# A two-layer hybrid decoder trunk: one written order for three engines through both routers

## The chip, the cores and the metric

The kernel runs on one core of one Trainium2 chip. The metric is the device time of one execution in microseconds (us). The kernel before took 904.0 us, the median of three runs (903.87 to 907.41). Its profiled execution took 905.78 us by the same clock and shows a span of 904.1 us, at a mean granted TensorE clock of 0.985.

## The reference, cut to what matters

256 tokens of width 1024 pass through two layers. Each layer is a mixer (layer 0 an mLSTM block, layer 1 a block-sparse attention) and a mixture of experts with 16 experts, two per token, chosen inside one group of four. Every sublayer ends in a layer normalisation.

```
x = layer_norm(ALPHA * x + gate * mixer(modulate(x)), ln_g, ln_b)
# router, on h = modulate(x, shift, scale)
probs  = softmax(h @ w_router)
scores = (probs + b_router).reshape(T, 4, 4)
group  = argmax over groups of the sum of the two best scores in the group
idx    = the two best experts of that group;  w = probs[idx] / sum(probs[idx])
# experts
y = sum over idx of w * ((silu(h @ w_gate[e]) * (h @ w_up[e])) @ w_down[e])
x = layer_norm(ALPHA * x + gate * y, ln_g, ln_b)
```

The shift, scale and gate vectors come from one condition vector through a matrix `w_ada` of 14 column blocks of 1024.

## The kernel before, in words

**The stream of weights.** All weights come from HBM in pieces of 0.5 MB, issued by SP in the order of their use into a ring of buffers (20 pieces, and 18 more during a mixture of experts). A piece is issued when the buffer it takes has been read for the last time. The experts' weights of one layer are 192 pieces.

**The end of a mixer.** The last part of the output projection (`y` in layer 0, `by` in layer 1) adds into four PSUM banks, one for each half of each of the two 128-token tiles. In layer 0 it is 48 matmuls of 128x512, from `wout_part` with h == 3 (L939 on); in layer 1 it stands just ahead of the last call of `moe` (L1539 on). Every product is three matmuls of high and low parts (`mm3`, L274 to L276). Written ahead of them is `before_moe` (L473): it finishes three condition vectors and folds the router's weights with one of them. On DVE, `adacc` sums a condition vector in eight passes over 128x1024 (L362), then PE sums over the partitions (`adaps`, L368), ACT copies the result (`mr`) and PE turns it (`adat`, L348). `wrt` (DVE, L483) is the router's weights times scale and shift; `rb` (PE, L485) sums it over the partitions, and `wr` (L488) is the folded router. `adag` (L452, L455) are the banks of a gate row. `ada_all` drives what is left of these sums.

**The router** (`moe`, L974 on). The gated sum into the residual `xt` (L547, L548), the statistics of the normalisation, the transposes `th` with their copies `xT`, the logits `pr`, `lr`, `pl`, `lg`, the exponentials `pexp` on ACT (they need the Exp table of ACT, loaded at `preload`, L536), and some thirty small DVE steps that end in `mask` (L1065). From the mask PE counts the places (`pp`, L1071), DVE forms the places (`pos`) and the one-hot matrices (`onehot`, L1089), and PE gathers the tokens of four experts (`ga`) from the normalised rows, which are split into a high part `xh` (ACT) and a low part `xl` (DVE, L1017). The gathered tokens are scaled into `xe` (L525 on ACT, L523 on DVE, two blocks of 128 columns each in turn), and the first gate products `pg` follow, 32 matmuls. They are the first that read the experts' weights. `lnps` are banks with the normalisation's rows; from them DVE forms the start of the residual sum in eight passes (L1335, L1336). `mxi` is the number of tokens of the fullest expert; every engine reads it for a branch (L1338) to a part for overflowing experts.

**What sets the order.** A scheduler orders the instructions of each engine by readiness and priority. Where `pinned` is set on an engine's wrapper (`Ordered`, L117), an instruction keeps its place in program order against the others, and its line shows as L135. In the kernel before only PE is pinned, from the first gather (`ga`) on through the experts. The end of the mixer and the router are the scheduler's.

Of the kernel before, what the change touches and what calls it, by code (L numbers as in the profile page):

```python
# [21 lines left out]
NT = S // P  # L22
# [6 lines left out]
E = 16  # L29
# [128 lines left out]
def _body(ctx, tc, x, w_ada, a_w_in, a_wq, a_wk, a_wv, a_w_out, b_w_kv, b_wq, b_wo, moe_w_gate, moe_w_up,  # L158
          moe_w_down, pc, rows, cst, out):
    nc = tc.nc  # L160
    V, A, T = [Ordered(tc, e) for e in (nc.vector, nc.scalar, nc.tensor)]
# [3 lines left out]
    small = ctx.enter_context(tc.tile_pool(name="small", bufs=2))  # L165
# [10 lines left out]
    def bankB(name):  # L176
        return psB.tile([P, 512], F32, tag="B", name=name)
# [11 lines left out]
    def C(name):  # L189
        g, o, w = CS[name]  # L190
        return cs[g][:, o:o + w]
# [15 lines left out]
    count = [0]  # L207
# [336 lines left out]
    def add_gated(t, o, n, y, gate, name, dst=xt):  # L544
        c = slice(o, o + n)
        tmp = small.tile([P, 512], F32, tag="lntmp", name=f"lntmp{name}{t}{o}")[:, 0:n]
        V.tensor_tensor(tmp, y, gate[:, c], op=OP.mult)  # L547
        V.tensor_tensor(dst[:, t, c], dst[:, t, c], tmp, op=OP.add)  # L548

    def ln_stats(src, t, name):  # L550

        st = small.tile([P, 4, 6], F32, tag="lnst", name=f"lnst{name}{t}")
        mv = small.tile([P, 2], F32, tag="lnmv", name=f"lnmv{name}{t}")
        rs = small.tile([P, 1], F32, tag="lnrs", name=f"lnrs{name}{t}")
        for i in range(4):
# [5 lines left out]
    def normalise(src, t, st, on_act=False):  # L561
        if on_act:
            nb = small.tile([P, 1], F32, tag="lnnb", name=f"lnnb{count[0]}_{t}")
            V.scalar_tensor_tensor(nb, st[0], -1.0, st[1], op0=OP.mult, op1=OP.mult)
            return A.activation(xt[:, t, :], src[:, t, :], AF.Identity, bias=nb, scale=st[1])
# [373 lines left out]
    def wout_part(h, w, ahl):  # L939
        ws = {}  # L940
        late = pe.tile([P, 2, 2, 512], F32R, tag="hh", name="wlate") if h == 3 else None
        for hf in range(2):
            for k in range(0, 4, 2):
                pump()
                pump()
                ws[k, hf], ws[k + 1, hf] = split(wsp, w[hf][:, k:k + 2, :], f"wo{h}_{k}{hf}", late if (k, hf) == (0, 0) else None)
            if h < 3:
                for t in range(NT):
                    for k in range(4):
                        mm3(yA[t][hf], tuple(a[:, k, P * t:P * t + P] for a in ahl), ws[k, hf], h == 0 and k == 0, False)  # L950
        if h == 3:
            gate = before_moe(0)
            ada_all()
            for t in range(NT):
                for hf in range(2):
                    for k in range(4):
                        mm3(yA[t][hf], tuple(a[:, k, P * t:P * t + P] for a in ahl), ws[k, hf], False, k == 3)
            return gate
# [15 lines left out]
    def moe(layer, y, gate1, last):  # L974
        ln0 = 2 * layer
        jm = 6 * layer + 3
        with ExitStack() as mc:
# [8 lines left out]
            xh = pm.tile([P, NT, D], F32R, name=f"xh{layer}")  # L986
            xl = pm.tile([P, NT, D], F32R, name=f"xl{layer}")
            lg = pm.tile([P, NT, E], F32, name=f"lg{layer}")
            for t in range(NT):
                for h in range(2):  # L990
                    add_gated(t, 512 * h, 512, y[t][h], gate1, f"m{layer}")
                for h in range(2):
                    pt = bankB(f"th{layer}_{t}{h}")
                    for k in range(4):
                        T.transpose(pt[:, P * k:P * k + P], xt[:, t, 512 * h + P * k:512 * h + P * k + P], ident)
                    A.copy(xT[:, t, 4 * h:4 * h + 4, :], pt.rearrange("p (k s) -> p k s", k=4))
                pr = bankB(f"pr{layer}_{t}")
# [3 lines left out]
                lr = small.tile([P, P], F32, tag="cv", name=f"lr{layer}_{t}")  # L1001
                V.tensor_copy(lr, pr[:, 0:P])
                T.matmul(pl[:, E * t:E * t + E], lr, C("selr"), start=True, stop=True)
                st = ln_stats(xt, t, f"m{layer}")
                V.scalar_tensor_tensor(lg[:, t, :], pl[:, E * t:E * t + E], st[1], rb[:, E:], op0=OP.mult, op1=OP.add)
                if t:
                    end = preload(AF.Exp)
                normalise(xt, t, st, t == 0)

            def split_x(t):  # L1010
                with tc.issue_after(end):
                    A.copy(xh[:, t, :], xt[:, t, :])

            def low_part(t):
                for h in range(2):
                    c = slice(512 * h, 512 * h + 512)
                    V.tensor_tensor(xl[:, t, c], xt[:, t, c], xh[:, t, c].bitcast(F32), op=OP.subtract)  # L1017

            split_x(0)

            def sm(nm, shape, dt=F32):
                return pm.tile([P] + shape, dt, name=f"{nm}_{layer}")

            def bc(t, n):
                return t.unsqueeze(len(t.shape)).to_broadcast(list(t.shape) + [n])
# [4 lines left out]
            ss = sm("ss", [NT, E])  # L1030
            V.tensor_reduce(s1, lg, axis=AX.X, op=OP.max, negate=True)
            for t in range(NT):
                end = A.activation(pe[:, t, :], lg[:, t, :], AF.Exp, bias=s1[:, t:t + 1], accum_out=s2[:, t:t + 1]).ins
            split_x(1)

            rows_ = [ln_bank(ln0, q, h, bankA) for h in range(2) for q in range(2)]
            gate = gate_rows(jm + 2)
# [16 lines left out]
            V.tensor_reduce(gs.rearrange("p t g -> p (t g)"), pairs, axis=AX.X, op=OP.max)  # L1054
            gl = sm("gl", [NT, NG, 3])
            gn = sm("gn", [NT, NG])
            losses(gl, gs)
            V.tensor_reduce(gn, gl, axis=AX.X, op=OP.add)
            el = sm("el", [NT * NG, 4, 3])
            en = sm("en", [NT * NG, 4])  # L1060
            losses(el, g4)
            V.tensor_reduce(en, el, axis=AX.X, op=OP.add)
            V.tensor_scalar(en, en, 1.5, None, op0=OP.is_lt)
            mask = sm("mask", [NT, E], BF16)
            V.scalar_tensor_tensor(mask.rearrange("p t (g j) -> p (t g) j", g=NG), bc(gn.rearrange("p t g -> p (t g)"), 4), 0.5, en,  # L1065
# [36 lines left out]
            wide = sm("wide", [NT, P + 2 * E], F32R)  # L1102
            for t in range(NT):
                V.tensor_copy(wide[:, t, 0:P], ident)
# [430 lines left out]
            wps[k, hf], wps[k + 1, hf] = split(wsp, w[hf](k), f"bo{hf}_{k}", None if hf else late[(k - 4) // 2])  # L1535
    gate = before_moe(1)
    ada_all()
    for t in range(NT):
# [46 lines left out]
```

## Time and profile before

| | |
|---|---|
| median of three runs | 904.0 us (903.87 to 907.41) |
| profiled execution: its time, its span | 905.78 us, 904.1 us |
| PE busy | 858.2 us (95%) |
| DVE, ACT busy | 529.1 us (59%), 331.4 us (37%) |
| weights and inputs read | 316.53 MB, 351 GB/s over the span |
| the chain that ended last | PE 40%, DMA 10%, DVE 3%, ACT 2% |

Busy shares are means over stages with different limits. PE counts as busy while it holds a matmul, also when its clock is low or when it goes no faster than the weights come. So the stages are read one by one: layer 0's mixer ends near 293 us, its experts run from 317 to 522 us, mixer 1 to 662 us, its experts from 681 us to the end.

### The profile page before, as it was taken

How to read it: one execution, taken by the hardware profiler on the slowest of the kernel's cores; microseconds unless marked ns; L12 is line 12 of the kernel's file. 1: busy time of each engine (PE TensorE's matmuls, PEld its weight loads, DVE VectorE, ACT ScalarE, POOL GpSimd, SP SyncE). 2: the span in 40 equal slices, each digit the busy share in tenths (PEclk: the TensorE clock that was granted, in tenths of full speed). 3: DMA queues.
4: the chain of work that ended last, by engine and by line, in shares of the span. 5: the costliest groups of instructions: out<-in, count | busy, mean ns of one | idle time of the engine just before them, and what ended most of it. 6: DMA issues, size and time to landing. Idle time of an engine off the chain costs nothing.

```text
span 904.1 us, 13441 instructions
## 1 busy us (share of the span) xinstructions
PE 858.2 (95%) x5049; PEld 533.3 (59%) x5052; DVE 529.1 (59%) x963; ACT 331.4 (37%) x550; POOL 7.8 (1%) x21
## 2 busy tenths in 40 slices
PE   8998999998999799999999889999979999999994
PEld 4887998786887434334343369877754443434332
DVE  2469997587878824332333289999983323333317
ACT  3458665357564411112111036576652111101020
POOL 0020000000000000000000000000000000000000
PEclk9999999999999899999999999999989999999998
DMA  9999886798868999999999999976997999999993
GB/s 326 393 386 355 293 330 205 273 411 324 307 227 275 381 333 407 407 407 406 408 406 407 377 387 412 400 284 238 361 338 262 407 407 407 407 407 407 407 400 121
DMA packets 161921, 318.56 MB, mean 352 GB/s; under 512 B 10120, under 2 KB 28168, under 8 KB 161848
## 3 DMA queue, kind: packets, MB, share of 16 engines
q1 hardware_dynamic: 161704, 317.42, 93.5%
q8 instruction: 42, 0.69, 0.3%
q14 instruction: 31, 0.25, 0.1%
q10 hardware_dynamic: 144, 0.20, 0.1%
HBM read 316.53 MB, written 1.05 MB: 351 GB/s over the span
## 4 chain that ended last, share of the span: by engine, by line
PE 40%; DMA 10%; DVE 3%; ACT 2%; issue 1%; DVEq 0%; SPq 0%; ACTq 0%
PE py L135 8%; PE pg L135 8%; PE pu L135 7%; DMA w<-in_moe_w_up_dram 3%; DMA w<-in_moe_w_down_dram 3%; PE ga L135 3%; PE po L135 2%; DMA ada<-in_w_ada_dram 2%; DMA w<-in_moe_w_gate_dram 1%; PE bo L1477 1%; PE bk L275 1%; PE by L274 1%; PE bk L276 1%; PE bk L274 1%; PE by L276 1%
## 5 line engine op out<-in xcount | busy, mean ns | idle before, releaser
L1238 DVE SCALAR_TENSOR_TENSOR yl<-py,wsl,yh 128x512 fp32r<-128x512 f32 x28 | 21.0, 750 | 171.2 <-ACT yh L1237 171.2
L135 PE MATMUL py<-w,aT 128*64 128x512 f32 (+1 forms) x576 | 118.3, 548 | 1.8 <-DMA w<-in_moe_w_down_dram 1.8
L135 PE MATMUL pu<-w,xe 128*64 128x512 f32 x512 | 118.8, 596 | 0.2 <-DMA w<-in_moe_w_up_dram 0.2
L135 PE MATMUL pg<-w,xe 128*64 128x512 f32 x512 | 116.1, 596 | 0.0
L362 DVE SCALAR_TENSOR_TENSOR adacc<-ada,pk,adacc 128x1024 f32<-128x1024 f32 x70 | 89.4, 1278 | 0.4
L135 PEld LDWEIGHTS py<-w,aT 128*64 128x64 f32 x576 | 41.3, 137 | 74.4 <-issue 58.8
L135 PEld LDWEIGHTS pu<-w,xe 128*64 128x64 f32 x512 | 36.1, 137 | 67.5 <-issue 61.2
L135 PEld LDWEIGHTS pg<-w,xe 128*64 128x64 f32 x512 | 34.8, 137 | 63.9 <-issue 58.9
L1204 ACT COPY aT<-aT 128x512 f32<-128x512 f32 x16 | 9.4, 586 | 139.5 <-PE aT L135 139.5
L547 DVE TENSOR_TENSOR lntmpe<-po,gate 128x512 f32<-128x512 f32 x56 | 36.1, 685 | 41.3 <-PE po L135 41.3
L1237 ACT ACTIVATE yh<-py,wsl 128x512 fp32r<-128x512 f32 x28 | 19.2, 687 | 84.2 <-PE py L135 84.2
L525 ACT ACTIVATE xe<-ga,coef 128x256 f32<-128x256 f32 x32 | 16.1, 562 | 73.0 <-PE ga L135 63.0
L274 PE MATMUL z<-hh,wz 128*128 128x256 f32 x128 | 36.7, 287 | 0.0
L276 PE MATMUL z<-hh,wz 128*128 128x256 f32 x128 | 36.2, 283 | 0.0
L275 PE MATMUL z<-hl,wz 128*128 128x256 f32 x128 | 36.1, 282 | 0.0
L548 DVE TENSOR_TENSOR xt<-xt,lntmpe 128x512 f32<-128x512 f32 x56 | 36.0, 683 | 0.0
L1197 DVE TENSOR_TENSOR a<-a,pu 128x512 f32<-128x512 f32 x16 | 11.0, 689 | 36.4 <-PE pu L135 20.3
L135 PE MATMUL ga<-onehot,xh 128*128 128x256 f32 x128 | 31.8, 327 | 0.0
L135 PE MATMUL xm<-hh,win 128*128 128x256 f32 x144 | 28.9, 290 | 0.7 <-ACT hh L135 0.7
L1192 ACT ACTIVATE a<-pg 128x512 f32<-128x512 f32 x16 | 9.6, 597 | 52.2 <-PE pg L135 52.2
L135 PEld LDWEIGHTS ga<-onehot,xh 128*128 128x128 f32 x128 | 25.3, 223 | 5.6 <-DVE xt L548 4.1
L135 PE MATMUL ga<-onehot,xl 128*128 128x256 f32 x128 | 27.7, 283 | 0.0
(387 smaller groups left out, 1892.9 us busy)
## 6 DMA issues: line engine op xcount, KB each, us to landing
w<-in_moe_w_gate_dram SPq DMA_DIRECT2D x128, 512.0 KB, 10.2
w<-in_moe_w_up_dram SPq DMA_DIRECT2D x128, 512.0 KB, 10.2
w<-in_moe_w_down_dram SPq DMA_DIRECT2D x128, 512.0 KB, 10.2
ada<-in_w_ada_dram SPq DMA_DIRECT2D x112, 512.0 KB, 9.2
win<-in_a_w_in_dram SPq DMA_DIRECT2D x16, 512.0 KB, 8.4
wz<-in_a_w_in_dram SPq DMA_DIRECT2D x16, 512.0 KB, 7.5
wout<-in_a_w_out_dram SPq DMA_DIRECT2D x16, 512.0 KB, 10.1
wv<-in_a_wv_dram SPq DMA_DIRECT2D x8, 512.0 KB, 5.8
```

The costliest lines, as they stand in the source:

```text
L135: return self.tc.keep_in_program_order(f(*a, **kw))
L274: T.matmul(ps, l[0], r[0], start=start, stop=False, skip_group_check=True)
L275: T.matmul(ps, l[0], r[1], start=False, stop=False, skip_group_check=True)
L276: T.matmul(ps, l[1], r[0], start=False, stop=stop, skip_group_check=True)
L362: V.scalar_tensor_tensor(acc, w, c, acc, op0=OP.mult, op1=OP.add)
L525: A.activation(dst, ps, AF.Identity, bias=sh[:, k:k + 1], scale=sc[:, k:k + 1])
L547: V.tensor_tensor(tmp, y, gate[:, c], op=OP.mult)
L548: V.tensor_tensor(dst[:, t, c], dst[:, t, c], tmp, op=OP.add)
L1192: A.activation(a, pg, AF.Silu)
L1197: V.tensor_tensor(a, a, pu, op=OP.mult)
L1237: A.activation(yh, py, AF.Copy, scale=wsl[:, b:b + 1])
L1238: V.scalar_tensor_tensor(yl, py, wsl[:, b:b + 1], yh.bitcast(F32), op0=OP.mult, op1=OP.subtract)
```

## The change

From the last products of a mixer to the high and low parts of the router's weights `W`, the instructions of PE, DVE and ACT keep the order in which the code writes them. For PE the flag is set ahead of the last products of each mixer; for DVE and ACT from the first gated sum of the router to `wide`. Inside, some steps are written in other places: the two tiles' transposes, logits and sums stand interleaved; the normalisation of `xt` is written after the exponentials (tile 1) and after the first one-hot (tile 0); tile 0's high part is formed by ACT straight from the unnormalised row, with bias and scale; the low parts and the normalisation of `W` stand behind the first one-hot; the copies of the identity into `wide` stand ahead of the router; the order of two groups of comparisons is exchanged.

```diff
@@ wout_part, h == 3 (and the same line ahead of the last products of mixer 1)
             gate = before_moe(0)
             ada_all()
+            T.pinned = True
             for t in range(NT):
@@ moe
+            for t in range(NT):
+                V.tensor_copy(wide[:, t, 0:P], ident)
+            V.pinned = A.pinned = T.pinned = True
...
             for t in range(NT):
                 for h in range(2):
                     add_gated(t, 512 * h, 512, y[t][h], gate1, f"m{layer}")
+                    if (t, h) == (1, 0):
+                        V.reciprocal(rs[0], rs[0])
+                        V.scalar_tensor_tensor(nb, mv[0][:, 0:1], -1.0, rs[0], op0=OP.mult, op1=OP.mult)
+                    for i in range(2 * h, 2 * h + 2):
+                        V.bn_stats(st[t][:, i, :], xt[:, t, 256 * i:256 * i + 256])
+                V.bn_aggr(mv[t], st[t])
+                if t == 0:
+                    A.activation(rs[0], mv[0][:, 1:2], AF.Sqrt, bias=epsc)
...
+            A.activation(rs[1], mv[1][:, 1:2], AF.Sqrt, bias=epsc)
+            A.activation(warm, epsc, AF.Exp)
...
-                if t:
-                    end = preload(AF.Exp)
-                normalise(xt, t, st, t == 0)
...
-            split_x(0)
...
             for t in range(NT):
-                end = A.activation(pe[:, t, :], lg[:, t, :], AF.Exp, ...)
-            split_x(1)
+                A.activation(pe[:, t, :], lg[:, t, :], AF.Exp, ...)
+            normalise(xt, 1, (mv[1][:, 0:1], rs[1]))
+            A.activation(xh[:, 0, :], xt[:, 0, :], AF.Identity, bias=nb, scale=rs[0])
+            A.copy(xh[:, 1, :], xt[:, 1, :])
...
-            V.tensor_reduce(s1, W, axis=AX.X, op=OP.add)
-            V.reciprocal(s1, s1)
-            V.tensor_tensor(W, W, bc(s1, E), op=OP.mult)
...
+            onehot(0)
+            normalise(xt, 0, (mv[0][:, 0:1], rs[0]))
             low_part(0)
-            placed = onehot(0)
-            with tc.issue_after(placed):
-                low_part(1)
+            placed = low_part(1)
+            V.tensor_reduce(s1, W, axis=AX.X, op=OP.add)
+            V.reciprocal(s1, s1)
+            V.tensor_tensor(W, W, bc(s1, E), op=OP.mult)
...
+            V.pinned = A.pinned = T.pinned = False
```

PE's queue at the end of mixer 0, in the kernel before (av, axc: the activations' parts; wlate, wo: parts of the output weights; adaps and adat are the next condition vector's sum and turn):

```order
L455 MATMUL adag_1_2998<-mr_1781,pick 128x512
L274 MATMUL y_0_2289<-wlate,av_2851 128x512
...
L275 MATMUL y_1_2290<-wo_21_2990,av_2851 128x512
L485 MATMUL rb_3009<-wrt_3006,ones 128x256
L276 MATMUL y_1_2290<-wo_21_2990,axc_2852 128x512
...
L276 MATMUL y_1_2292<-wo_21_2990,axc_2852 128x512
L368 MATMUL adaps_3022<-adacc_2926,ones 32x256 x4
L502 MATMUL lnps_0_0_3235<-lnr,pick 128x512
L348 MATMUL adat_3029<-cs,mr_3027 128x128 x2
```

The same place in the changed kernel:

```order
L455 MATMUL adag_1_2998<-mr_1781,pick 128x512
L485 MATMUL rb_3009<-wrt_3006,ones 128x256
L368 MATMUL adaps_3022<-adacc_2926,ones 32x256 x4
L348 MATMUL adat_3029<-cs,mr_3027 128x128 x2
L135 MATMUL y_0_2289<-wlate,av_2851 128x512 x2
L135 MATMUL y_0_2289<-wlate,axc_2852 128x512
...
L135 MATMUL y_1_2292<-wo_21_2990,axc_2852 128x512
L135 MATMUL th_00_3174<-cs,xt 128x128 x4
```

`rb`, `adaps` and `adat` stood among and behind the 48 `y` products; now they stand ahead of all of them.

PE's queue at the end of mixer 1, in the kernel before (kT_wo, vv_wo, bo: parts of the output weights):

```order
L276 MATMUL by_1_6169<-bo_2_6253,ol__5275 128x512
L274 MATMUL by_1_6171<-bo_2_6253,oh__5274 128x512
...
L485 MATMUL rb_6352<-wrt_6349,ones 128x256
L368 MATMUL adaps_6356<-adacc_6210,ones 32x256 x4
...
L276 MATMUL by_1_6171<-bo_6_6331,ol__5275 128x512
```

In the changed kernel:

```order
L455 MATMUL adag_1_6340<-mr_5465,pick 128x256 x2
L485 MATMUL rb_6352<-wrt_6349,ones 128x256
L368 MATMUL adaps_6356<-adacc_6210,ones 32x256 x4
L135 MATMUL by_0_6168<-kT_wo,oh__5274 128x512 x2
L135 MATMUL by_0_6168<-kT_wo,ol__5275 128x512
...
L135 MATMUL by_1_6171<-bo_6_6331,ol__5275 128x512
```

Here too `rb` and `adaps` went from among the last products to a place ahead of all 48 that read kT_wo, vv_wo, bo_4 and bo_6.

DVE's queue behind the mask of layer 0, in the kernel before (L1335 and L1336 are the passes of the residual sum, L523 the scaling of gathered tokens):

```order
L1083 TENSOR_TENSOR pos_3294<-pos_3294,pp_3288 128x32
L1080 TENSOR_REDUCE s_0_3228<-W_3296 128x2
...
L1089 TENSOR_TENSOR onehot_0_3304<-pos_3294,cs 128x256
L1017 TENSOR_TENSOR xl_3137<-xt,xh_3136 128x512 x2
L1100 CAST mxi_3311<-mxc_3309 128x1
...
L1336 SCALAR_TENSOR_TENSOR xt<-lnps_1_0_3237,xt 128x512 x2
L523 TENSOR_SCALAR xe_0_3390<-ga_0_1_3392,coef 128x256 x2
L523 TENSOR_SCALAR xe_0_3390<-ga_0_3_3394,coef 128x256 x2
L1335 SCALAR_TENSOR_TENSOR xt<-xt,lnps_0_1_3239 128x512 x2
```

In the changed kernel (the passes are L1348 and L1349 there):

```order
L135 TENSOR_TENSOR onehot_0_3301<-pos_3296,cs 128x256 x2
L135 TENSOR_SCALAR xt<-xt,lnmv_0_3144,lnrs_0_3146 128x1024
L135 TENSOR_TENSOR xl_3137<-xt,xh_3136 128x512 x4
L135 TENSOR_REDUCE s_0_3228<-W_3298 128x2
...
L1349 SCALAR_TENSOR_TENSOR xt<-lnps_1_0_3239,xt 128x512
L135 CAST mxi_3314<-mxc_3312 128x1
...
L1348 SCALAR_TENSOR_TENSOR xt<-xt,lnps_0_1_3241 128x512 x2
L1349 SCALAR_TENSOR_TENSOR xt<-lnps_1_1_3243,xt 128x512
L523 TENSOR_SCALAR xe_0_3390<-ga_0_1_3392,coef 128x256 x2
L523 TENSOR_SCALAR xe_0_3390<-ga_0_3_3394,coef 128x256 x2
```

Behind the one-hot now stand one normalisation, four low parts instead of two, and seven of the eight passes of the residual sum ahead of the first `xe` of DVE, where there were four. `mxi` has gone behind three of the passes.

## Rows read from the trace of the kernel before

**Rows 1.** The chain that ended last, in order of time: start us, length us, what

```profile
502.56 10.90 DMA w<-in_moe_w_down_dram
```

**Rows 2.** Stretches of 20 us: busy us by engine, PEclk, DMA share, GB/s

```profile
340.00:360.00 20.00, 20.00 (x108) 9.99 (x106) 9.27 (x18) 3.42 (x6) 0.00 (x0) 1.00 1.05 407
...
600.00:620.00 20.00, 19.61 (x132) 16.53 (x131) 19.50 (x33) 11.78 (x31) 0.00 (x0) 1.00 0.65 229
```

**Rows 3.** Timeline of PE, end of mixer 0: start us, length us, instruction

```profile
281.58 0.40 PE L274 MATMUL y<-wlate,av 128*128 128x512 f32 x1
...
289.27 0.59 PE L485 MATMUL rb<-wrt,ones 128*128 128x256 f32 x2
...
292.97 0.40 PE L276 MATMUL y<-wo,axc 128*128 128x512 f32 x1
...
293.29 0.64 PE L368 MATMUL adaps<-adacc,ones 128*32 128x256 f32 x8
...
294.48 0.44 PE L348 MATMUL adat<-cs,mr 128*128 128x128 f32 x2
```

**Rows 4.** Timeline of DVE, the same stretch

```profile
288.33 0.49 DVE L483 TENSOR_TENSOR wrt<-pk,coef 128x128 f32<-128x128 f32 x2
...
291.66 1.28 DVE L362 SCALAR_TENSOR_TENSOR adacc<-ada,pk,adacc 128x1024 f32<-128x1024 f32 x1
```

**Rows 5.** Timeline of PE, end of mixer 1

```profile
649.95 0.40 PE L276 MATMUL by<-kT_wo,ol__5275 128*128 128x512 f32 x1
...
656.99 0.59 PE L485 MATMUL rb<-wrt,ones 128*128 128x256 f32 x2
...
661.42 0.39 PE L276 MATMUL by<-bo,ol__5275 128*128 128x512 f32 x1
```

**Rows 6.** Timeline of DVE, the same stretch of layer 1

```profile
651.48 1.28 DVE L362 SCALAR_TENSOR_TENSOR adacc<-ada,pk,adacc 128x1024 f32<-128x1024 f32 x1
...
656.18 0.48 DVE L483 TENSOR_TENSOR wrt<-pk,coef 128x128 f32<-128x128 f32 x2
```

**Rows 7.** Timeline of PE, router of layer 0, the wait for the mask

```profile
309.26 0.20 PE L1071 MATMUL pp<-mask,before 128*128 128x16 bf16 x1 [5.07 <-DVE mask L1065]
...
309.42 1.87 PE L331 MATMUL warmg<-onesq 128*128 128x512 bf16 x4
```

**Rows 8.** Stretches of 1 us, router of layer 0, columns as above

```profile
308.00:309.00 1.00, 0.00 (x0) 0.00 (x0) 0.94 (x10) 0.00 (x0) 0.00 (x0) 0.50 1.05 408
...
314.00:315.00 1.00, 1.00 (x8) 1.00 (x7) 0.80 (x2) 0.00 (x0) 0.00 (x0) 0.70 1.06 410
```

**Rows 9.** Timeline of PE, first gather (layer 1) and first gate products (both)

```profile
316.57 7.09 PE L135 MATMUL pg<-w,xe 128*64 128x512 f32 x32
...
675.44 3.98 PE L135 MATMUL ga<-onehot,xh 128*128 128x256 f32 x16
...
681.49 7.09 PE L135 MATMUL pg<-w,xe 128*64 128x512 f32 x32
```

**Rows 10.** Timeline of ACT, router of layer 1

```profile
662.29 1.08 ACT L996 COPY xT<-th 128x512 f32<-128x512 f32 x2 [1.44 <-PE th L995]
...
677.22 1.28 ACT L536 ACT_TABLE_LOAD   x1 [5.14 <-DVE wide L1105]
```

**Rows 11.** Timeline of DVE, router of layer 1

```profile
671.17 0.17 DVE L1038 RECIPROCAL s<-s 128x2 f32<-128x2 f32 x1 [0.16 <-ACT pexp L1033]
...
674.72 0.40 DVE L1089 TENSOR_TENSOR onehot<-pos,cs 128x256 fp32r<-128x256 f32 x1
...
675.48 1.29 DVE L1017 TENSOR_TENSOR xl<-xt,xh 128x512 fp32r<-128x512 f32 x2
```

**Rows 12.** Groups by line, DVE, 300 to 321 us: count, busy us, mean ns

```profile
L1335 DVE SCALAR_TENSOR_TENSOR xt<-xt,lnps 128x512 f32<-128x512 f32 x4 | 2.6, 681 | 0.0
...
L566 DVE TENSOR_SCALAR xt<-xt,lnmvm,lnrsm 128x1024 f32<-128x1024 f32 x1 | 0.8, 804 | 0.0
```

**Rows 13.** Stretches of 5 us, start of the experts of layer 0

```profile
315.00:320.00 5.00, 5.00 (x30) 2.63 (x30) 4.28 (x8) 3.22 (x5) 0.00 (x0) 1.00 0.54 199
```

More of the change, by code (lines that the diff above doesn't have):

```diff
@@ L559, in ln_stats, with normalise @@
         return mv[:, 0:1], rs
[L561 to L565, printed above, removed]
+    def normalise(src, t, st):
         return V.tensor_scalar(xt[:, t, :], src[:, t, :], st[0], st[1], op0=OP.subtract, op1=OP.mult)
@@ L988, in moe @@
             lg = pm.tile([P, NT, E], F32, name=f"lg{layer}")
+            wide = pm.tile([P, NT, P + 2 * E], F32R, name=f"wide_{layer}")
+            for t in range(NT):
+                V.tensor_copy(wide[:, t, 0:P], ident)
+            V.pinned = A.pinned = T.pinned = True
+            st = [small.tile([P, 4, 6], F32, tag="lnst", name=f"lnst{layer}_{t}") for t in range(NT)]
+            mv = [small.tile([P, 2], F32, tag="lnmv", name=f"lnmv{layer}_{t}") for t in range(NT)]
+            rs = [small.tile([P, 1], F32, tag="lnrs", name=f"lnrs{layer}_{t}") for t in range(NT)]
+            nb = small.tile([P, 1], F32, tag="lnnb", name=f"lnnb{layer}")
             for t in range(NT):
@@ L991, in moe @@
                     add_gated(t, 512 * h, 512, y[t][h], gate1, f"m{layer}")
+                    if (t, h) == (1, 0):
[6 more added lines that the diff above has]
+                    A.activation(rs[0], mv[0][:, 1:2], AF.Sqrt, bias=epsc)
+            for t in range(NT):
                 for h in range(2):
-                    pt = bankB(f"th{layer}_{t}{h}")
+                    pt = (bankB, bankA)[t](f"th{layer}_{t}{h}")
                     for k in range(4):
@@ L996, in moe @@
                     A.copy(xT[:, t, 4 * h:4 * h + 4, :], pt.rearrange("p (k s) -> p k s", k=4))
+            A.activation(rs[1], mv[1][:, 1:2], AF.Sqrt, bias=epsc)
+            A.activation(warm, epsc, AF.Exp)
+            lr = []
+            for t in range(NT):
                 pr = bankB(f"pr{layer}_{t}")
@@ L1000, in moe @@
                         T.matmul(pr[32 * g:32 * g + 32, 0:P], wr[:, E * (4 * i + g):E * (4 * i + g) + 32], xT[:, t, 4 * i + g, :], start=(i == 0), stop=(i == 1))
[L1001 to L1005, printed above, removed]
-                if t:
-                    end = preload(AF.Exp)
-                normalise(xt, t, st, t == 0)
-            def split_x(t):
-                with tc.issue_after(end):
-                    A.copy(xh[:, t, :], xt[:, t, :])
+                lr.append(small.tile([P, P], F32, tag="cv", name=f"lr{layer}_{t}"))
+                V.tensor_copy(lr[t], pr[:, 0:P])
+                if t == 0:
+                    V.reciprocal(rs[1], rs[1])
+            for t in range(NT):
+                T.matmul(pl[:, E * t:E * t + E], lr[t], C("selr"), start=True, stop=True)
+                V.scalar_tensor_tensor(lg[:, t, :], pl[:, E * t:E * t + E], rs[t], rb[:, E:], op0=OP.mult, op1=OP.add)
             def low_part(t):
@@ L1016, in low_part @@
                     c = slice(512 * h, 512 * h + 512)
-                    V.tensor_tensor(xl[:, t, c], xt[:, t, c], xh[:, t, c].bitcast(F32), op=OP.subtract)
-            split_x(0)
+                    ins = V.tensor_tensor(xl[:, t, c], xt[:, t, c], xh[:, t, c].bitcast(F32), op=OP.subtract)
+                return ins.ins
             def sm(nm, shape, dt=F32):
@@ L1032, in moe @@
             for t in range(NT):
-                end = A.activation(pe[:, t, :], lg[:, t, :], AF.Exp, bias=s1[:, t:t + 1], accum_out=s2[:, t:t + 1]).ins
-            split_x(1)
+                A.activation(pe[:, t, :], lg[:, t, :], AF.Exp, bias=s1[:, t:t + 1], accum_out=s2[:, t:t + 1])
+            normalise(xt, 1, (mv[1][:, 0:1], rs[1]))
+            A.activation(xh[:, 0, :], xt[:, 0, :], AF.Identity, bias=nb, scale=rs[0])
+            A.copy(xh[:, 1, :], xt[:, 1, :])
             rows_ = [ln_bank(ln0, q, h, bankA) for h in range(2) for q in range(2)]
@@ L1053, in moe @@
             gs = sm("gs", [NT, NG])
-            V.tensor_reduce(gs.rearrange("p t g -> p (t g)"), pairs, axis=AX.X, op=OP.max)
             gl = sm("gl", [NT, NG, 3])
             gn = sm("gn", [NT, NG])
-            losses(gl, gs)
-            V.tensor_reduce(gn, gl, axis=AX.X, op=OP.add)
             el = sm("el", [NT * NG, 4, 3])
             en = sm("en", [NT * NG, 4])
+            V.tensor_reduce(gs.rearrange("p t g -> p (t g)"), pairs, axis=AX.X, op=OP.max)
             losses(el, g4)
+            losses(gl, gs)
             V.tensor_reduce(en, el, axis=AX.X, op=OP.add)
+            V.tensor_reduce(gn, gl, axis=AX.X, op=OP.add)
             V.tensor_scalar(en, en, 1.5, None, op0=OP.is_lt)
@@ L1100, in moe @@
             V.tensor_copy(mxi, mxc)
-            wide = sm("wide", [NT, P + 2 * E], F32R)
-            for t in range(NT):
-                V.tensor_copy(wide[:, t, 0:P], ident)
             V.tensor_copy(wide[:, :, P:P + E], W)
             V.tensor_tensor(wide[:, :, P + E:], W, wide[:, :, P:P + E].bitcast(F32), op=OP.subtract)
+            V.pinned = A.pinned = T.pinned = False
             W2 = sm("W2", [NT, E])
@@ L1537, in _body @@
     ada_all()
+    T.pinned = True
     for t in range(NT):
```

## The prediction

> **What bounds the kernel now.** I read the chain of waits first, then stretches of 20 us, and then the timelines of PE, DVE and ACT around the two routers. The chain is held by PE in the mixers and by the transfers of expert weights in the experts: it waits 10.90 us on a piece of the last down weights of layer 0 [rows 1]. In the experts PE counts as busy all the time, but the stream moves 407 GB/s in a stretch like 340 to 360 us [rows 2], the highest level that lasts, so the stream sets the pace there. An expert stage therefore ends a fixed time after the stream gets going again behind the router. In mixer 1 it is the reverse: PE has 19.61 of 20 us and the stream only 229 GB/s [rows 2].
>
> Between mixer and experts the stream runs on into the ring, then waits, since a buffer comes free only when a gate product has read it. In layer 0 the ring is full just as `pg` starts at 316.57, and 315 to 320 us moves 199 GB/s [rows 9, 13]. So the one number that counts at each router is the start of `pg`: 316.57 in layer 0, 681.49 in layer 1 [rows 9]. What delays it in layer 0 goes through the experts at the stream's pace, through a mixer bound by PE, and to the end; what delays it in layer 1 goes to the end as it is. I write e for the end of the last output product: 293.37 in layer 0 and 661.81 in layer 1 [rows 3, 5]. Now `pg` stands at e+23.2 and e+19.68.
>
> **The flag ahead of the last products.** This is the costly part. In the queue of before, `y` follows the gate row directly and starts at 281.58; `rb`, whose operand `wrt` is written by DVE at 288.33, is fitted in among the products at 289.27; `adaps` at 293.29 and `adat` at 294.48 come behind the last of them, at 292.97 [rows 3, 4]. In the changed queue the three stand ahead of all 48 products. Their operands don't come sooner: DVE has no gap up to there, and its order up to the last `adacc` (291.66 plus 1.28, so 292.94) is the same [rows 4]. `adaps` then starts at about 293.3, ACT copies, and `adat` ends its two products at about 294.7. Queued behind them is every `y`, although its data is there; ACT, DVE and the router wait for `y`. From 281.58 to 292.97 there are 47 products and two slots for `rb`: 11.39/49 = 0.232 us each. The last product starts at 294.7 + 47 x 0.232 = 305.6 in place of 292.97: 12.6 us later.
>
> In layer 1, `by` starts at 649.95, `rb` comes at 656.99 and the last product at 661.42 [rows 5]. `wrt` comes at 656.18 [rows 6]; three passes of the gated sum (0.6 each) stood ahead of it on DVE, and these can't run now because their banks aren't finished. So `wrt` comes at about 654.3 and `adaps` is done at about 655.9; the last `adacc` (two passes of 1.28 from 651.48 on) is no later. All 48 products that stand behind then take 47 x 0.231 = 10.85 us: the last starts at 666.75, which is 5.3 us later.
>
> **The clock in the hold.** While PE waited 5.07 us for the mask, its granted clock went to .50, the lower of its two levels (1.2 GHz), by 308, and it came back only in the slice from 314 (.70, so at about 314.6), some 5.3 us after work began again at 309.26 [rows 7, 8]. The holds are longer, with only `rb` inside. So I let the products begin at half rate: 2.5 us are lost in layer 0, where `adaps` puts PE to work a little ahead of `y`, and 2.0 in layer 1, where `rb` and `adaps` do so 1.2 us ahead of `by`. The bounds are 0 (the clock doesn't fall) and all products at half rate, 48 x 0.232 = 11.1 per layer. I take the values near the measured return. The end e moves by 15.1 and 7.3 us.
>
> **The shorter router.** After e, the chain loses the first tile's turn: its sums, transposes and statistics are now done while the last `y` products run. What is left is about 1.3 (last gated sum), 1.6 (transposes and copies), 1.5 (`pr`, `lr`, `pl`, `lg`) and 0.7 (maximum, exponentials), so e+5.1. The Exp table (1.28, the length of the load at 677.22 [rows 10]) is loaded behind the last copy at about e+3.2 and ends beside the maximum. From the reciprocal behind the exponentials to the one-hot it was 674.72 - 671.17 = 3.55 [rows 11]; the three steps of the normalisation of `W`, 0.1 each, move out of it partly, and the one-hot begins at about e+8.65. The first gather product follows 0.7 later, as from 674.72 to 675.44 [rows 9, 11]: e+9.4, against 675.44 - 661.81 = e+13.6 before.
>
> But `pg` doesn't wait for the gather alone. DVE's half of `xe` is queued behind the two one-hots (0.8), a normalisation of 0.8 [rows 12], four low parts at 0.6 (two took 1.29 [rows 11]), seven of the eight passes of the residual sum (681 ns [rows 12], 0.62 with their overlap) and nine small steps at 0.1. That is 8.65 + 0.8 + 0.75 + 2.4 + 4.3 + 0.9 = e+17.8; the first of these `xe` blocks is there at e+18.3. ACT's two blocks feed a quarter of the 7.09 us of `pg` [rows 9] before, so `pg` runs as if started at e+18.3-1.8 = e+16.5. In layer 0 that is 6.65 earlier relative to e than before.
>
> In layer 1, ACT must read the overflow count `mxi` ahead of its table load and its own `xe`. That load started 5.14 us after ACT was free, behind `wide` in time [rows 10]. `mxi` now comes three passes and several small steps behind the low parts, at about e+15.1; a table load of 1.28, a small activation and the first block of 0.55 bring `pg` to e+17.55: a gain of 2.1 against e+19.68. The bounds are 0 and the 4.2 that the first gather gains.
>
> **What costs nothing.** The copies of the identity (0.2 each), `nb` and the reciprocals lie in DVE's wait for the first output bank. ACT forms tile 0's high part straight from `xt` (one pass in place of two) while DVE does the mask; it would cost its length if the mask came sooner than e+8. The gate row's two ACT passes end before the gather needs ACT. The exchanged comparisons are the same count. SP also reads `mxi`, now just ahead of the first weight load that waits for a gate product; `mxi` at e+15.1 is earlier than any free buffer, so 0, at most about 1 us if pieces came free sooner.
>
> **The sum.** Layer 0: 15.1 - 6.65 = +8.45. Layer 1: 7.3 - 2.1 = +5.2. Together +13.65 on the profiled execution's 905.78 us, 919.4. That execution is 1.8 above the median; on the median of 904.0 it makes 917.7, the prediction.
>
> **A rule against the trace.** While `pp` waited for the mask, the warming products behind it, which read only a constant, waited too: they start at 309.42, right behind `pp` at 309.26 [rows 7]. The Trainium skill says the same (PSUM — Partial Sum Buffer, Engine vs sequencer instructions): matmuls start and complete in program order. By it the sum stands at 917.7; were `y` free to pass `rb`, it would be rival B's. No row shows a product that passed a waiting one.
>
> **The rivals.** A is the forecast.
>
> B, faster: the products aren't held, because the data of `rb` and `adaps` comes sooner than I read, and the shorter router counts. Then layer 0 gains what the stream stood idle, at least (407 - 199)/407 x 5 = 2.6 us [rows 2, 13], and layer 1 gains 2.1: 904.0 - 4.7 = 899.3. For it speaks only that the router's chain is shorter; against it stand the rows of `wrt` and `adacc`. Chance 7%. It decides from `adaps` at under 284 in layer 0.
>
> C: the clock doesn't fall in the holds, or `rb` in their middle keeps it up: 917.7 - 4.5 = 913.2. For it, `rb` splits the hold; against it, 5.07 us sufficed [rows 7, 8]. 25%.
>
> D: the delay of layer 0 is caught up in mixer 1, whose stream has room (229 GB/s [rows 2]): only layer 1's 5.2 remain, 909.2. Against it, PE is the bound there and starts late. 8%.
>
> E: the held products all run at half rate: 8.6 more in each layer, 934.9. Against it, the clock came back in 5.3 us. 3%.
>
> F: the router loses a further DVE or ACT wait that I cost at nothing, or gains less: the first 0 to 4 us above A, up to 921.9. It is part of A's own range, 913 to 922.
>
> **How the numbers follow.** A with F has 52%, C 25%, D 8%, B 7%, E 3%, and 5% is for a case between no change and D, a hold hidden for the greater part. About 0.5% (4.5 us) is what a measurement of this kernel can tell from no change. B is the only faster case: 0.07. The same: 0.06, from that 5% and the edge of B. Slower: 0.87. The range of 8 in 10 is 908 to 922.5: it takes in A, C and D, and leaves out B, E and A's upper edge.
>
> **What would show it.** In the timeline of PE: `rb` at about 289.3 with nothing of `y` ahead of it, then `adaps`, `adat`, and the first `y` at about 294.7; a granted clock of .50 in the 1-us stretches around 288 to 298 and at about 653 to 660; the last `y` at about 308, the last `by` 7 us later relative to the start of its gate row. In the router: almost no wait of PE for the mask, the first gather at e+9.4, seven passes of the residual sum ahead of DVE's first `xe`, the start of `pg` at about 324 to 325 with a gap inside, and the stream back at 407 GB/s about 8 us later than before in layer 0 and 13 to 14 in layer 1. The prediction is wrong if `y` starts near 282, if `pg` follows its e by much more or less than 16.5 to 17.5, or if mixer 1 ends less late than it starts.

## The result, and the profile after

| | kernel before | changed kernel |
|---|---|---|
| median | 905.42 us (903.87 to 907.41, 4 runs) | 930.19 us (929.27 to 931.43, 4 runs) |
| ratio | | 1.0263 (95%: 1.0240 to 1.0286) |
| profiled execution, span | 905.78, 904.1 us | 931.43, 929.8 us |
| PE, DVE, ACT busy | 858.2, 529.1, 331.4 us | 868.1, 533.9, 329.4 us |
| mean granted clock | 0.985 | 0.969 |

The change made the kernel slower by 24.8 us in the medians. The prediction had the direction and 13.7 us. PE was busy 9.9 us longer with the same 5049 matmuls, at a lower mean clock; DVE and ACT hardly changed. The rest of the 25.7 us between the spans is waiting.

The end of mixer 0 in the changed kernel, timeline of PE (start us, length us), for [rows 3]:

```profile
285.09 0.40 PE L455 MATMUL adag<-mr,pick 128*128 128x512 f32 x1
292.71 1.19 PE L485 MATMUL rb<-wrt,ones 128*128 128x256 f32 x2 [7.22 <-DVE wrt L483]
296.75 1.08 PE L368 MATMUL adaps<-adacc,ones 128*32 128x256 f32 x8 [2.85 <-DVE adacc L362]
298.37 0.69 PE L348 MATMUL adat<-cs,mr 128*128 128x128 f32 x2 [0.54 <-ACT mr L343]
298.71 1.20 PE L135 MATMUL y<-wlate,av 128*128 128x512 f32 x2
...
311.30 0.40 PE L135 MATMUL y<-wo,axc 128*128 128x512 f32 x1
```

This is the hold as forecast: after the gate row PE does nothing for 7.22 us, then 2.85, then 0.54, and the first `y` starts 13.62 us behind the gate row in place of 0.23. The two stretches of 2 us (last three columns: granted clock, DMA share, GB/s) show its clock:

```profile
300.00:302.00 2.00, 2.00 (x6) 1.52 (x6) 0.22 (x2) 0.00 (x0) 0.00 (x0) 0.50 1.00 385
302.00:304.00 2.00, 2.00 (x10) 1.65 (x9) 0.66 (x1) 0.00 (x0) 0.00 (x0) 0.97 1.04 400
```

The first products run at the lower level (1.2 GHz), and the clock is back at about 302. The last `y` ends at 311.70, which is e here.

In layer 0's router PE shows a wait that the kernel before does not have. There the first 16 gather products ran in one piece, at the lower clock:

```profile
310.72 3.98 PE L135 MATMUL ga<-onehot,xh 128*128 128x256 f32 x16
```

In the changed kernel they don't, and DVE shows what they wait for:

```profile
321.19 1.82 PE L135 MATMUL ga<-onehot,xh 128*128 128x256 f32 x12
326.23 1.23 PE L135 MATMUL ga<-onehot,xh 128*128 128x256 f32 x4 [3.21 <-DVE mxc L135]
327.25 3.03 PE L135 MATMUL ga<-onehot,xl 128*128 128x256 f32 x16
330.22 7.09 PE L135 MATMUL pg<-w,xe 128*64 128x512 f32 x32
```

```profile
325.32 0.67 DVE L1348 SCALAR_TENSOR_TENSOR xt<-xt,lnps 128x512 f32<-128x512 f32 x1
325.91 0.18 DVE L135 TENSOR_TENSOR W<-W,s 128x32 f32<-128x32 f32 x1
326.01 0.17 DVE L135 TENSOR_REDUCE mxc<-pp 128x1 f32<-128x16 f32 x1
...
329.47 1.89 DVE L523 TENSOR_SCALAR xe<-ga,coef 128x256 f32<-128x256 f32 x4
```

The gather starts at e+9.5, as forecast (e+9.4), and stops before its fourth bank until `mxc`, the last step that reads `pp`, is done. DVE's `xe` starts at 329.47 = e+17.8, also as forecast, but the gather itself ends only at about 330.2. The wait of 3.21 us also lowers the granted clock, to 0.50 in the next stretch of 2 us:

```profile
326.00:328.00 2.00, 1.77 (x8) 1.77 (x9) 2.00 (x9) 0.00 (x0) 0.00 (x0) 0.50 0.00 0
```

In layer 1 the same wait comes again, and there is one more. PE's rows answer to [rows 5, 9], DVE's to [rows 6, 11]:

```profile
668.22 1.19 PE L485 MATMUL rb<-wrt,ones 128*128 128x256 f32 x2 [4.92 <-DVE wrt L483]
669.34 1.08 PE L368 MATMUL adaps<-adacc,ones 128*32 128x256 f32 x8
670.36 1.22 PE L135 MATMUL by<-kT_wo,oh__5274 128*128 128x512 f32 x2
...
678.85 0.39 PE L135 MATMUL by<-kT_wo,ol__5275 128*128 128x512 f32 x1
...
682.93 0.39 PE L135 MATMUL by<-bo,ol__5275 128*128 128x512 f32 x1
...
702.12 1.22 PE L135 MATMUL ga<-onehot,xh 128*128 128x256 f32 x4 [3.21 <-DVE mxc L135]
...
706.68 7.88 PE L135 MATMUL pg<-w,xe 128*64 128x512 f32 x32
```

```profile
679.28 0.36 DVE L989 CAST wide<-cs 128x128 fp32r<-128x128 f32 x2 [7.89 <-PE by L135]
679.55 0.68 DVE L135 TENSOR_TENSOR lntmpm<-by,gate 128x512 f32<-128x512 f32 x1
...
686.98 0.69 DVE L135 TENSOR_TENSOR xt<-xt,lntmpm 128x512 f32<-128x512 f32 x1
```

`wide` copies a constant. It can't wait for data; it starts at 679.28, when the last product that reads kT_wo (678.85 and 0.39 long) is over. The first gated sum is queued behind it, and the last one ends at e+4.4, where I had e+1.3. Behind the wait for `mxc` the first gate products `pg` took 7.88 us in place of 7.09, at a granted clock of 0.50 from 702 to 708.

**Where the time lies.** Counted from the last matmul of the gate row (281.35 and 649.72 before), which is just ahead of everything that the change moves on PE; all differences of starts and ends in the timelines of PE:

| us | layer 0: to e | e to pg | both | layer 1: to e | e to pg | both |
|---|---|---|---|---|---|---|
| before | 12.02 | 23.20 | 35.22 | 12.09 | 19.68 | 31.77 |
| changed | 26.61 | 18.52 | 45.13 | 20.41 | 23.36 | 43.77 |
| forecast difference | +15.1 | -6.65 | +8.45 | +7.3 | -2.1 | +5.2 |
| measured difference | +14.6 | -4.7 | +9.9 | +8.3 | +3.7 | +12.0 |

The two come to 21.9 us. The spans differ by 25.7, because in the profiled execution of before the gate row comes 3.74 us sooner. Up to there the two kernels issue the same PE instructions, so that part is no effect of the order (the last section tells what most of it is). The delay of layer 0's `pg`, 13.65 with those 3.74, is 13.19 at mixer 1's gate row: mixer 1 hands it on.

### The profile page after: what moved, and what is told of

Read it like the earlier page. It is cut to its first block, busy times and chain, and to the rows that moved or that the text cites. A ratio compares the mean times of both kernels' runs of the same rounds, so it can differ in the third digit from the quotient of the medians.

```text
span 929.8 us, 13430 instructions
## 1 busy us (share of the span) xinstructions
PE 868.1 (93%) x5049; PEld 541.5 (58%) x5052; DVE 533.9 (57%) x965; ACT 329.4 (35%) x548; POOL 7.8 (1%) x21
## 4 chain that ended last, share of the span: by engine, by line
PE 42%; DMA 5%; DVE 4%; ACT 2%; issue 1%; SPq 0%; DVEq 0%; ACTq 0%
PE py L135 9%; PE pg L135 8%; PE pu L135 8%; PE po L135 3%; PE ga L135 3%; DMA w<-in_moe_w_down_dram 2%; DMA w<-in_moe_w_up_dram 2%; DMA ada<-in_w_ada_dram 1%; PE bo L1490 1%; PE by L135 1%; PE bk L275 1%; PE bk L274 1%; PE bk L276 1%; PE aT L135 1%; PE s L1458 1%
## 5 line engine op out<-in xcount | busy, mean ns | idle before, releaser
L135 PEld LDWEIGHTS ga<-onehot,xh 128*128 128x128 f32 x128 | 23.1, 197 | 12.7 <-DVE mxc L135 6.8
L135 PE MATMUL ga<-onehot,xl 128*128 128x256 f32 x128 | 29.9, 309 | 0.0
L135 PE MATMUL xm<-hh,win 128*128 128x256 f32 x144 | 28.8, 289 | 0.7 <-ACT hh L135 0.7
```

The lines of the kernel that those rows point to most:

```text
L135: return self.tc.keep_in_program_order(f(*a, **kw))
```

## The experiments

H: the hold of the last products costs the time. R: the new order inside the router costs it. P: the gather waits for the bank of `pp`. W: `wide` holds up layer 1's sums. The kernel before was timed beside each group again. In e7 the gate row itself stands behind the first six of the last products in layer 0 and the first seven in layer 1, so that its columns count from a later place than the others.

| run | layer 0: to e, e to pg, both | layer 1: to e, e to pg, both | median | ratio (95%) |
|---|---|---|---|---|
| e1_free_y | 12.03, 29.10, 41.13 | 12.10, 23.01, 35.11 | 918.03 | 1.0134 (1.0111 to 1.0157) |
| e2_wide_back | 26.61, 18.51, 45.12 | 20.23, 18.61, 38.84 | 924.49 | 1.0198 (1.0181 to 1.0215) |
| e3_mxc_first | 26.32, 14.37, 40.69 | 19.54, 20.09, 39.63 | 920.28 | 1.0152 (1.0135 to 1.0169) |
| e4_pin_alone | 26.49, 19.43, 45.92 | 19.19, 18.81, 38.00 | 925.14 | 1.0203 (1.0186 to 1.0220) |
| e5_wide_mxc | 26.41, 14.36, 40.77 | 19.51, 14.37, 33.88 | 915.55 | 1.0091 (1.0056 to 1.0126) |
| e6_free_wide_mxc | 12.01, 25.28, 37.29 | 12.10, 16.65, 28.75 | 905.83 | 0.9992 (0.9973 to 1.0010) |
| e7_y_first | 15.68, 24.39, 40.07 | 9.71, 24.69, 34.40 | 917.83 | 1.0121 (1.0090 to 1.0153) |
| e8_before_warm | 12.01, 22.05, 34.06 | 12.12, 19.90, 32.02 | 907.15 | 1.0006 (0.9984 to 1.0028) |
| e9_layer1_only | 12.00, 23.13, 35.13 | 12.10, 18.28, 30.38 | 905.21 | 0.9979 (0.9964 to 0.9995) |
| e10_layer1_warm0 | 12.00, 22.11, 34.11 | 12.10, 16.63, 28.73 | 905.15 | 0.9978 (0.9964 to 0.9993) |
| e11_split_by | 12.01, 23.14, 35.15 | gate row among the products | 905.10 | 0.9972 (0.9958 to 0.9985) |

**e1: both flags ahead of the last products taken out.**

```diff
             ada_all()
-            T.pinned = True
             for t in range(NT):
```

> The changed kernel without the two flags ahead of the mixers' last products: rb, adaps and adat stand among and behind them again, all else as changed. Theory H (the hold of the last products costs the time: in the traces the last product ends 14.6 us later in layer 0 and 8.3 us later in layer 1, counted from the gate row): the time falls by 22 to 28 us, to 902 to 908, and if the shorter router then counts it lies below the kernel before. Rival R (the new order inside the router costs the time): it stays above 918.

918.03: at R's edge, and 10 us above H's range. The hold is gone (12.03 and 12.10 to e), and that is worth 12 us. But the written router alone is 11 us slower than the scheduler's: +5.9 and +3.3 to `pg`. Timeline of DVE, layer 0 of e1, where e is at 294.87:

```profile
296.46 0.17 DVE L350 TENSOR_TENSOR mod<-adat,pk 128x8 f32<-128x8 f32 x1 [2.02 <-PE adat L348]
...
296.81 0.68 DVE L135 TENSOR_TENSOR lntmpm<-y,gate 128x512 f32<-128x512 f32 x1
...
304.98 0.75 DVE L135 BATCH_NORM_STATS2 lnst<-xt 128x6 f32<-128x256 f32 x2
```

In the kernel before, the scheduler began the sums at 292.86, 11.5 us behind the gate row, and put tile 0's logits between tile 1's sums. Here they begin 14.0 us behind it, as DVE first waits 2.02 us for `adat`. In the written order the four sums with their statistics stand in one piece of 8.9 us ahead of every later step of DVE, and in layer 0 of e1 nothing of it runs beside the products. So part of what the prediction calls the shorter router is there only behind the hold, whose products come bank by bank and cover the first sums. Both theories hold in part: the hold and the written router each cost time.

**e2: the identity copies put back.**

```diff
-            for t in range(NT):
-                V.tensor_copy(wide[:, t, 0:P], ident)
             V.pinned = A.pinned = T.pinned = True
...
             V.tensor_copy(mxi, mxc)
+            for t in range(NT):
+                V.tensor_copy(wide[:, t, 0:P], ident)
```

> The changed kernel with the two copies of the identity into wide put back behind mxi. Theory W (in layer 1 these copies wait on DVE for output products that read kT_wo, whose memory they take, and hold up the gated sums: 7.89 us idle up to 679.28, last sum at e+4.4 in place of e+1.3): about 3 us less, 927. Rival: the sums wait for the output banks anyway, and the time stays at 930.

W holds, and for more than I said: layer 0 doesn't move (18.51), layer 1's `pg` comes 4.75 us sooner (18.61 for 23.36). DVE there now waits for the first output bank, which it needs, for 3.61 us in place of 7.89:

```profile
673.03 0.69 DVE L135 TENSOR_TENSOR lntmpm<-by,gate 128x512 f32<-128x512 f32 x1 [3.61 <-PE by L135]
```

**e3: the maximum of the counts ahead of the one-hot.**

```diff
+            mxc = sm("mxc", [1])
+            V.tensor_reduce(mxc, pp[:, 2 * E:3 * E], axis=AX.X, op=OP.max)
             onehot(0)
```

> The changed kernel with the maximum of the counts (mxc, the last reader of the bank pp) written ahead of the first one-hot; the scheduler then also puts DVE's xe ahead of six of the eight passes of the residual sum. Theory P (the fourth gather bank is pp's and waits 3.21 us for mxc in each layer): the gather runs without a gap, pg starts at about e+14 in place of e+18.5 in layer 0 and some 4 us sooner in layer 1: 922 to 924. Rival (the low parts or the read of mxi on ACT hold pg as long): 928 to 930.

P holds: the gather of layer 0 runs without the wait for `mxc`, and `pg` starts at e+14.37, 4.15 us sooner. In layer 1 it is 3.3 us, with `wide` still in the way. The time, 920.28, lies below the range I gave. But the edit frees more than the bank. In layer 0 the scheduler now puts DVE's first `xe` behind one pass of the residual sum, where seven stood, and in layer 1 ACT scales its blocks (693.23) ahead of the table load (695.18), where the changed kernel has them behind it (703.26 and 704.66). Timeline of PE, layer 0 of e3 (e at 309.01; the window ends behind 12 of the 32 `pg`):

```profile
318.50 2.30 PE L135 MATMUL ga<-onehot,xh 128*128 128x256 f32 x16
...
323.38 2.79 PE L135 MATMUL pg<-w,xe 128*64 128x512 f32 x12
```

**e4: the kernel before with the flag on the last products alone** (the added line of the change, and `T.pinned = False` behind the products).

> The kernel before with only the flag on the mixers' last products (and taken off behind them); the router's order is the scheduler's. Theory H: +14.6 and +8.3 at the end of the products, less some 5 and 3 us for the first tile's sums and transposes, which now run beside the products: 918 to 924. Rival R: no slower than 907.

925.14, a little above H's upper end. The hold appears without any other part of the change: the first `y` 13.63 us behind the gate row, e at 26.49 and 19.19. The first tile's sums beside the products give back 3.8 in layer 0 and 0.9 in layer 1, less than the 5 and 3 I wrote down.

**e5: e2 and e3 together.**

> The changed kernel with both mends together: the identity copies behind mxi, and mxc ahead of the first one-hot; the flags ahead of the last products stay. Theory S (the loss is hold plus bank wait plus wide wait): each mend keeps its worth, 4.15 us in layer 0, and in layer 1 4.75 plus about 4, so 916 to 918, and what is left against the kernel before, about 9 to 11, is the hold less the shorter router, as the prediction's own sum (13.65) had it. Rival: the two waits cover each other in layer 1, and the time stays at 919 to 921.

915.55, just under S's range. Both routers now take the same time, 14.36 and 14.37, so moving `mxc` is worth 4.15 us in layer 0 and 18.61 - 14.37 = 4.24 in layer 1, and moving the copies into `wide` 4.75. The three make 13.1 of the 14.6 us between the medians of the changed kernel and e5. What is left, 9.2 us against the kernel before, is hold less shorter router.

**e6: e5 without the flags ahead of the last products.**

> As e5, and without the flags ahead of the last products. Theory S: e1's 918 less about 4.2 in layer 0 and 4 in layer 1: 909 to 911, no faster than the kernel before, because the written order of the sums on DVE (all four ahead of the router's first step) costs what the other steps save. Rival: the shorter router now shows, 900 to 905.

Neither: 905.83, the same as before. Layer 0 loses 2.1 us and layer 1 gains 3.0. In layer 1 the sums start 4.4 us ahead of e, beside the last products. In layer 0 DVE is busy with the condition vector up to 0.4 us ahead of e and then waits 2.00 us for `adat`, whose result stands ahead of the sums.

**e7: the last products written ahead of the gate row, rb, adaps and adat.**

> As e5, but the last products stand ahead of rb, adaps and adat in the code, so that they keep their order bank by bank and wait for nothing. Theory H: no hold, the last product ends about 12 us after the gate row's place as in the kernel before, in both layers; the sums on DVE start only behind the last condition vector. 904 to 910. Rival R (the written order of the router is the cost): above 914.

A miss for H, 917.83. In layer 0 products still wait, now for one of their own operands, and e lies 3.7 us farther behind the gate row than in the kernel before (timeline of PE):

```profile
287.44 0.73 PE L135 MATMUL y<-wo,av 128*128 128x512 f32 x2 [2.93 <-ACT av L270]
288.66 0.49 PE L135 MATMUL y<-wo,axc 128*128 128x512 f32 x1 [0.49 <-DVE axc L271]
```

In layer 1 no product waits. In both layers `rb` now does: it stands behind all products, and the sums on DVE come only behind `rb` (timeline of DVE, layer 1; 6.22 us in layer 0):

```profile
668.25 0.42 DVE L486 TENSOR_REDUCE rb<-rb 128x32 f32<-128x256 f32 x1 [6.63 <-PE rb L485]
...
669.65 0.69 DVE L135 TENSOR_TENSOR lntmpm<-by,gate 128x512 f32<-128x512 f32 x1
```

The wait of the queue on PE became one of the queue on DVE. R's number is met, but the router is not the cause: e6 has the same one and came to 905.83.

**e8: the kernel before, `WARM = 15, 4` in place of `5, 4`.**

> The kernel before with 15 in place of 5 matmuls on a constant ahead of the counts. Theory C (the low clock behind PE's wait for the mask costs the first gather): PE idles 2.5 and 0.6 us in place of 5.07 and 3.12, the granted clock stays at 1.00, and pg comes 2 us sooner relative to the mask in each layer: 903 against 907. Rival: the stream or DVE holds pg anyway, or the products delay the counts: 906 to 908.

The same time. PE's wait for the mask in layer 0 fell from 5.07 to 2.89 us [rows 7], and still the granted clock went down (stretches of 2 us):

```profile
310.00:312.00 2.00, 0.00 (x0) 0.00 (x0) 1.93 (x20) 0.51 (x1) 0.00 (x0) 0.91 1.05 407
312.00:314.00 2.00, 1.68 (x10) 0.85 (x10) 1.85 (x12) 0.00 (x0) 0.00 (x0) 0.50 1.06 410
```

So the theory of this run was not tested as meant: the clock fell in spite of the added work. `pg` gains 1.16 us in layer 0 and loses 0.25 in layer 1, where the counts start at 678.28 right behind the added products: these delay them, as the rival has it. The median shows neither.

**e9, e10, e11: versions built from what held.** e9 is the kernel before with e6's router in layer 1 alone:

```diff
     end = moe(0, yA, gate, False)
...
-    moe(1, yB, gate, True)
+    moe_1(1, yB, gate, True)
```

> The kernel before with e6's router in layer 1 alone; layer 0 and the last products of both mixers as before. Theory S: layer 1's pg comes at 28.8 us behind the gate row in place of 31.8, and layer 0 keeps 35.2 (e6 had 37.3): 3 us less than the kernel before, a ratio of 0.996 to 0.998. Rival: the end is held by the stream, and the ratio is 0.999 to 1.001.

> As e9, with 15 constant matmuls ahead of the counts in layer 0 (5 before). If the clock of the first gather in layer 0 counts: 1 us less than e9, a ratio of 0.995 to 0.997. Rival: no difference from e9, because the stream still has pieces to bring when pg starts.

e9 is faster than the kernel before by 1.7 us in the medians; its interval leaves 1 out, but reaches into the rival's band. Layer 1's `pg` came 30.4 us behind the gate row, not 28.8 as in e6 and e10, whose router there is the same code. The difference is the clock: from 671 to 673 us it was 0.50 in e9 and 1.00 in e10, and the same four products took 2.05 and 1.17 us (e9, then e10):

```profile
671.38 2.05 PE L135 MATMUL lnps<-lnr,pick 128*128 128x512 f32 x4
```

```profile
672.00 1.17 PE L135 MATMUL lnps<-lnr,pick 128*128 128x512 f32 x4
```

e10, with 15 constant products ahead of the counts in layer 0, has `pg` there 1.0 us sooner than e9, but its median can't be told from e9's. From layer 0's `pg` to layer 1's the two take nearly the same, 363.5 and 363.3 us (364.9 in the kernel before). e11 sets the wait of mixer 1 under work, with tile 0's products ahead of `rb` and `adaps` and tile 1's behind:

```diff
+    for t in range(NT):
+        if t == 1:
+            gate = before_moe(1)
+            ada_all()
+        T.pinned = True
         for hf in range(2):
             for k in range(4, KD):
                 wo_mm(t, hf, k, wps[k, hf])
+        T.pinned = False
```

> e9 with mixer 1's last products kept in order in two halves: tile 0's 24, then the gate row, rb and adaps, then tile 1's 24. Theory H turned to use: rb and adaps find their operands while tile 0's products run, so nothing is held (the last product ends 12 us behind, as before), and tile 0's sums run beside tile 1's products. Layer 1's pg then comes about 2 us sooner than in e9: ratio 0.994 to 0.997 against the kernel before. Rival: DVE reaches the sums no sooner (they stand behind wr in the order), or PE waits for wrt after all: 0.998 to 1.002.

```profile
657.02 0.39 PE L135 MATMUL by<-bo,ol__5275 128*128 128x512 f32 x1
657.25 0.59 PE L485 MATMUL rb<-wrt,ones 128*128 128x256 f32 x2
657.77 0.64 PE L368 MATMUL adaps<-adacc,ones 128*32 128x256 f32 x8
```

`rb` and `adaps` stand ahead of half of the products as in the changed kernel, and nothing is held. At 0.9972 it has the lowest ratio measured, 2 us under the kernel before. That it beats e9 is not shown: the intervals overlap, and from layer 0's `pg` to layer 1's the profiled execution takes 363.5 us as in e9, not 2 us less. Its router ran at 0.50 from 668 to 674, as e9's did.

## Why the prediction was wrong, point by point

By the rows of PE the sum is 8.3 us short (21.9 for 13.65): 0.5 in the hold, and 7.8 in the router (2.0 in layer 0, 5.8 in layer 1), where two waits were put at nothing. They are the third and the fourth point. The prediction had named the sign: `pg` followed its e by 18.5 and 23.4 us, not by 16.5 to 17.5.

- **Hold of the last products: right, in mechanism and size.** +14.6 and +8.3 against +15.1 and +7.3. In layer 1 it is 1.0 more, because `rb` and `adaps` themselves ran at the lower clock (1.19 and 1.08 us for 0.59 and 0.64). e4 shows the hold alone, e1 its absence. B is out: `adaps` started at 296.75.
- **Clock in the hold: right in kind, a little smaller.** From the first `y` to e it is 12.99 us in layer 0; at 0.232 a product and 0.40 for the last it would be 11.3, so 1.7 were lost, not 2.5. C and E are out.
- **"But pg doesn't wait for the gather alone": this step failed.** It lists what is queued on DVE ahead of `xe`, and e+17.8 was right to the tenth, by some luck: the one-hot began 0.3 us later than forecast and the queue behind it was 0.3 shorter. It leaves out what the moved `mxc` releases: the PSUM bank of `pp`, which the gather takes as its fourth. `mxc` went from right behind the counts to behind two passes of the residual sum. `pg` came at e+18.5 in place of e+16.5, 2.0 us that the sum lacks. e3 took off 4.15 us, part of which lay under DVE's queue, which e3 shortens as well. That ACT must read `mxi` ahead of its own `xe`, as forecast for layer 1, did not hold in e3 and e5.
- **"What costs nothing: the copies of the identity lie in DVE's wait for the first output bank": this step failed, and by most.** In layer 1 they wait themselves, up to the last read of kT_wo, and everything on DVE stands behind. 4.75 us by e2. Of the 6.8 us that layer 1 came out worse, 5.8 are the router (a loss of 3.7 for a gain of 2.1) and 1.0 the hold. What is left of the 5.8 beside `wide` is 1.1, with the wait for `mxc` in it. That the cause is the memory that `wide` takes over from kT_wo is inferred from the moment at which the wait ends, and from the code, which closes the pool of kT_wo just ahead of the router; e2 shows the cost of the place, not of the address.
- **The shorter router: right in the start of the gather (e+9.5); what it is worth hangs on the order in which its inputs come.** Behind the hold, with both waits mended, it gains 8.8 and 5.3 us (e5), more than the forecast 6.65 and 2.1. With the scheduler's products it costs 5.9 and 3.3 us (e1), and with both waits mended as well it still costs 2.1 in layer 0 but gains 3.0 in layer 1 (e6).
- **F: right in kind, too small.** It names a further wait costed at nothing, and allows 4 us. What the two waits brought came to 7.8. With both mended (e5) the time is 915.55, inside the range; the edits of e5 also shorten DVE's queue ahead of `xe`.
- **D, catching up in mixer 1: out.** 13.65 became 13.19.
- **`pg` as the one number that counts: right.** From layer 1's `pg` to the end all 13 profiled executions took 222.3 to 223.1 us. The 407 GB/s are not the highest level that lasts, though: from 540 to 580 us, ahead of layer 1's experts, the stream moved 411 and 412.
- **The base.** I put the sum on a median of three runs, 904.0; beside the four groups of experiments the kernel before had medians of 906.4 to 907.1 (7 to 23 runs). That is 2.4 to 3.1 of the 12.5 us by which the time missed.

Open: in e1, e4 and e5 the medians lie 1 to 2 us farther from the kernel before than their two columns add up to (9.25 and 11.0 in e1, 16.9 and 18.1 in e4, 7.7 and 9.2 in e5); in e2 and e3 they agree (17.0 and 17.5, 13.3 and 13.3). The columns leave out the way to layer 0's gate row (281.35 to 285.09 us in the 13 profiles) and that from layer 0's `pg` to layer 1's gate row (331.5 to 334.6, leaving out e7 and e11, whose gate row stands elsewhere). The rest between the spans lies there, in e4 for instance 1.5 and 1.1 us. That the medians differ by the same is not shown.

## What to carry to other kernels

An instruction written early in a fixed order makes all that is behind it wait for its operands, also when it has none that are new: list for each moved step not only what it reads, but whose memory it overwrites and whose bank its read sets free. When a queue is fixed, find the last operand to arrive and put it under work that needs nothing from it (e11, where nothing is held, though a gain over e9 is not shown), not ahead of that work or behind all of it (e7). And a shorter chain is worth what it is in the order in which its inputs arrive, so test it without the parts that change that order.

## What the runs showed of the hardware

The same instructions cost a different time from one execution to the next, by the clock that PE is granted behind a wait. Between 70 and 74 us PE has two short waits in both kernels alike, with some 0.87 us of products between them: 0.80 and 1.79 us in the profiled execution of before, 0.80 and 1.75 in that of the changed kernel. Behind them the one had the full clock, and the other ran at half of it until about 80 us (timeline of PE and stretch of 2 us of the kernel before, then the two of the changed kernel):

```profile
73.83 0.39 PE L275 MATMUL q<-cl,wq 128*128 128x256 f32 x1 [1.79 <-DVE cl L271]
```

```profile
74.00:76.00 2.00, 2.00 (x18) 2.00 (x19) 2.00 (x4) 2.00 (x5) 0.00 (x0) 1.00 1.03 412
```

```profile
74.03 0.58 PE L275 MATMUL q<-cl,wq 128*128 128x256 f32 x1 [1.75 <-DVE cl L271]
```

```profile
74.00:76.00 2.00, 1.97 (x9) 1.97 (x10) 2.00 (x4) 2.00 (x4) 0.00 (x0) 0.50 1.01 406
```

This is 2.7 of the 3.74 us between the gate rows of layer 0, which came at 281.35 in the one and 285.09 in the other, and between 282.7 and 284.8 in the profiles of the experiments (284.42 in e8, which is the kernel before up to layer 0's router). In all twelve other profiles the clock fell behind these waits; only the profiled execution of before kept it. So the execution in which the numbers of the prediction were read was, up to there, the luckiest of all that were profiled. How much of the spread of the kernel before, 903.5 to 911.1 us over 23 runs, comes from this wait is not shown.
